# Layer 0's attention: scaling the probabilities by the merge weights, values stationary, groups summed in PSUM

## The chip, the cores and the metric

The kernel runs on one core of one Trainium2 chip. Its engines have their own instruction queues, each in order: PE (TensorE, matrix products and transposes), DVE (VectorE), ACT (ScalarE), POOL (GpSimd) and SP (SyncE, which here issues nearly all DMA transfers). The metric is the device time of one execution in microseconds.

## The reference

Two layers on 1024 tokens of width 1024: dilated attention and an MLP, then gated linear attention and an MLP. The change lies in the first layer's attention, which has 8 heads of 128 features and, for each head, three groups with their own queries, keys and values:

```python
for g, (window, dil) in enumerate(((128, 1), (512, 4), (2048, 16))):
    q = apply_rope(qkv[:, :, g, 0], cos, sin) * (HEAD_DIM ** -0.5)
    k = apply_rope(qkv[:, :, g, 1], cos, sin)
    v = qkv[:, :, g, 2]
    o_g, lse_g = dilated_group_attention(q, k, v, dil, window // dil)   # softmax over a band of keys
    outs.append(o_g); lses.append(lse_g)
alpha = jax.nn.softmax(jnp.stack(lses, axis=0), axis=0)
o = jnp.sum(alpha[..., None] * jnp.stack(outs, axis=0), axis=0)
x = x + o.reshape(B, S, ATTN_WIDTH) @ w_out
```

A group of dilation 4 or 16 attends within residue classes of the tokens (4 classes of 256 tokens, 16 of 64). The three groups' outputs are merged with weights from their softmax denominators, token by token.

## The kernel before

The projections run as products of float32 values split into a high and a low part (three matmuls of 128x512 for one product). Values are projected first and stored in DRAM (`vscr`). Then a loop over 24 passes `p` (8 heads times 3 groups, `h, g = divmod(p, NG)`) projects queries and keys. `Heads.run_head(p)` issues 14 half products of six matmuls, and calls `advance()` after each. `advance()` moves a clock by one step and issues whatever stands in an agenda for that step: `at(step, function, rank)` puts it there, lower ranks first, rank 5 where none is given. All else in the stage is placed by this agenda, in steps from `c = 14 * p`: the copies and sums of the projection's PSUM banks (`keep`, `column`), the rotary products (`turn` inside `column`, four steps after it), the rounding of the next pass's weights (`stage`), and the attention of the pass before, which `follow(p - 1, c)` plans.

In `column` a half of the queries or keys is summed on DVE, and SP then moves its two halves of partitions into each other's place (`cw`), which the rotary product needs.

Attention of one group (`Attention`; `Classes` for group 2) takes four stages, j = 0 to 3. `scores` makes query-key products with tokens of a block on partitions (at steps 8, 10, 12 and 14; group 2 makes all its 16 small ones at step 8). `soft` takes each row's extreme on DVE and the exponential with its sum on ACT (steps 9, 11, 13, 15). `turn` transposes the probabilities on PE and copies them to SBUF on ACT. `values` multiplies them, as stationary operand, with the values. The result, tokens on partitions, goes with each row's sum and extreme to DRAM (`og`, rows of 130 numbers per token and group). For group 2 `turn` stands at step 18 and `values` at step 20.

The merge of a head (`plan_merges`) starts nine steps into the pass of the next head's group 1. For each half of the tokens it reads the rows of all three groups (`merge_load`), computes three weights per token (`merge_weights`, `merge_shares`, four steps after the read), scales twelve tiles on ACT (`merge_scale`), adds them on DVE (`merge_join`), and writes the joined head to `oscr`, tokens on partitions. The output projection, which needs features on partitions, turns the joined heads again on PE: heads 0 to 3 with `turn_eight`, heads 4 to 7 with `t_head`. The last head's attention and merge (`tail`) run inside the output projection, two agenda steps per block of twelve matmuls.

PSUM has eight banks (`bank`), SBUF pools have fixed numbers of buffers: `k4` 25 of 4 KB per partition, `t2` 8, `r6` 1, `h8` 12.

Of the kernel before, what the change touches and what calls it, by code (L numbers as in the profile page):

```python
# [19 lines left out]
P = 128  # L20
D = 1024
# [20 lines left out]
def hybrid_trunk(ctx, tc, x, norm_mix, norm_mlp, norm_fin, a_in, a_out, g_in, g_up, g_b, g_nw,  # L42
# [927 lines left out]
    og = [drp.tile([S, NG, HD + 2], F32, name=f"og{h}") for h in range(HEADS)]  # L970
    oscr = drp.tile([S, D], F32, name="oscr")
# [219 lines left out]
    class Attention:  # L1191
        def __init__(self, g, h, qT, kT):
            self.g, self.h, self.qT, self.kT, self.st = g, h, qT, kT, {}

        def scores(self, j):
            ps = bank("pS").rearrange("p (i k) -> p i k", i=2)
# [5 lines left out]
            self.st[j] = ps  # L1202

        def soft(self, j):
            ps = self.st[j]
            tile_ = k4([P, 2, 512], F32, "pt")
            pt = tile_[:, 0, :].rearrange("p (i k) -> p i k", i=2)
            if j % 2 == 0:
                self.row = t2([P, 4, HD + 2], F32, "orow")
            for i in range(2):  # L1210
                k0, n, m0 = keys_of(self.g, 2 * j + i)
                r = 2 * (j % 2) + i
                m = self.row[:, r, HD + 1:HD + 2]
                dve.tensor_tensor_reduce(pt[:, i, :128 * n], ps[:, i, :128 * n], masks[:, m0:m0 + 128 * n],
                                         -scale, 1e38, op0=OP.add, op1=OP.min, accum_out=m)
                act.activation(pt[:, i, :128 * n], pt[:, i, :128 * n], AF.Exp, scale=-1.0,
                               bias=m, accum_out=self.row[:, r, HD:HD + 1])
            self.st[j] = tile_, self.row

        def turn(self, j):  # L1220
            tile_, row = self.st[j]
            pt = tile_[:, 0, :].rearrange("p (i k) -> p i k", i=2)
            ps = bank("pP")
            n = 0
            for i in range(2):
                for s in range(keys_of(self.g, 2 * j + i)[1]):
                    pe.transpose(ps[:, 128 * n:128 * n + 128], pt[:, i, 128 * s:128 * s + 128], ident)  # L1227
                    n += 1
            act.activation(tile_[:, 1, :128 * n], ps[:, :128 * n], AF.Copy)

        def values(self, j):
            tile_, row = self.st.pop(j)
            g, h = self.g, self.h
            if j % 2 == 0:
                self.po = bank("pO").rearrange("p (b d) -> p b d", d=HD)
            po = self.po
            n = 0
            for i in range(2):
                k0, nk, _ = keys_of(g, 2 * j + i)
                for s in range(nk):  # L1240
                    pe.matmul(po[:, 2 * (j % 2) + i, :], tile_[:, 1, 128 * n:128 * n + 128], self.v[:, k0 // 128 + s, :],  # L1241
                              start=(s == 0), stop=(s == nk - 1))
                    n += 1
            if j % 2:
                act.activation(row[:, :, 0:HD], po, AF.Copy)
                to = og[h][:, g, :]
                if g == 0:
                    sp.dma_start(to.rearrange("(b p) c -> p b c", p=P)[:, 2 * j - 2:2 * j + 2, :], row)
                else:
                    for n in range(2):  # L1250
                        sp.dma_start(to.rearrange("(b p r) c -> r p b c", p=P, r=4)[j - 1 + n],
                                     row[:, 2 * n:2 * n + 2, :])

        def plan(self, c, points, turn, values):

            def get():
                self.v = load_values(self.g, self.h)
            at(c + points[0] - 2, get)
            for j in range(4):
                t = c + points[j]  # L1260
                at(t, lambda j=j: self.scores(j), 2)
                at(t + 1, lambda j=j: self.soft(j), 2)
                at(c + turn[j], lambda j=j: self.turn(j), 3)
                at(c + values[j], lambda j=j: self.values(j), 4)

    class Classes(Attention):


        def scores(self, j):
            if j:  # L1270
                return
            self.ps = bank("pS").rearrange("p (b k) -> p b k", k=64)
            for b in range(8):
                for e in range(2):
                    sl = slice(128 * b + 64 * e, 128 * b + 64 * e + 64)
                    pe.matmul(self.ps[64 * e:64 * e + 64, b, :], self.qT[:, sl], self.kT[:, sl], start=True, stop=True,
                              tile_position=(0, 64 * e))
            self.pt = k4([P, 2, 512], F32, "pt")
            self.rows = [t2([P, 4, HD + 2], F32, "orow") for _ in range(2)]

        def soft(self, j):
            pt = self.pt[:, 0, :].rearrange("p (b k) -> p b k", k=64)
            for q in range(2):
                b, row = 2 * j + q, self.rows[q]
                m = row[:, j, HD + 1:HD + 2]
# [1321 lines left out]
```

## Time and profile before

| | |
|---|---|
| runs, median of 3 | 2567.89 us (2567.67 to 2568.99) |
| profiled execution, its own time | 2567.73 us |
| its span, first to last instruction | 2565.9 us |
| busy PE / DVE / ACT in the span | 2556.3 / 1863.5 / 1285.0 us |
| granted TensorE clock | 0.999 of full speed |
| DMA traffic | 544.8 MB, mean 212 GB/s |
| layer 0's heads and output projection of heads 0 to 3 | about 255 to 898 us of the span |

Times in the rows are microseconds from the span's start. A timeline row has the start, the duration, the engine, the line, the operation and its operands (out, then in). Where a row is merged, x4 counts the instructions. A float32 matmul of two operands that are not split leaves two records. Matmuls overlap, so start to start tells what one costs better than its duration. In rows of a line the three numbers are least, median and longest time in ns, and "DMA to landing" is from issue to completion in us.

### The profile page before, as it was taken

The numbers are of one execution on the slowest core, as the hardware profiler recorded it, in microseconds if no ns is written. First come the engines' busy times: TensorE is split into PE (matmuls) and PEld (weight loads), VectorE is DVE, ScalarE is ACT, GpSimd is POOL, SyncE is SP. The second block draws the span as 40 slices with busy tenths as digits, with TensorE's granted clock in tenths as the row PEclk, the third lists the DMA queues.
The fourth block names the chain that finished last, engine by engine and source line by source line (L and its number), as shares of the span: only waits on it lengthen the run. The fifth ranks groups of instructions, "written<-read, shape, count | busy, mean of one in ns | idle before, by whom it ended". The sixth has DMA issues, their size and how long they took to land.

```text
span 2565.9 us, 34655 instructions
## 1 busy us (share of the span) xinstructions
PE 2556.3 (100%) x12583; PEld 2120.2 (83%) x12583; DVE 1863.5 (73%) x2988; ACT 1285.0 (50%) x2335; POOL 17.9 (1%) x26
## 2 busy tenths in 40 slices
PE   9999999999999999999999999999999999999998
PEld 7888888888888888888888888888888888888887
DVE  7766878888888766788668785786666666566666
ACT  7443455555555445566544553654335555553344
POOL 0000000000000000000000000100000000000000
PEclk9999999999999999999999999999999999999999
DMA  5785466655656747899888765777546644495543
GB/s 191 254 276 195 108 160 151 155 152 150 161 151 189 229 164 258 265 328 307 326 302 301 278 216 195 278 252 269 182 151 216 230 149 142 154 340 205 189 147 124
DMA packets 357276, 544.80 MB, mean 212 GB/s; under 512 B 24576, under 2 KB 181008, under 8 KB 357104
## 3 DMA queue, kind: packets, MB, share of 16 engines
q1 hardware_dynamic: 356800, 542.18, 64.4%
q8 instruction: 99, 1.62, 0.3%
q14 instruction: 73, 0.60, 0.1%
q10 hardware_dynamic: 304, 0.40, 0.0%
HBM read 339.39 MB, written 177.93 MB: 202 GB/s over the span
## 4 chain that ended last, share of the span: by engine, by line
PE 99%; ACT 1%; DVE 0%; issue 0%
PE pX L854 19%; PE pB L1959 14%; PE pV L854 13%; PE pA L1959 10%; PE pB L1066 8%; PE pY L854 6%; PE pZ L854 6%; PE pA L1066 6%; PE pd L196 2%; PE pd L198 2%; PE pd L197 2%; PE pO L1241 2%; PE pS L1200 2%; PE pP L1227 1%; PE pT L259 1%; PE pO L2430 1%
## 5 line engine op out<-in xcount | busy, mean ns | idle before, releaser
L1959 PE MATMUL pB<-dh 128*128 128x512 f32 x512 | 199.2, 389 | 0.0
L1959 PE MATMUL pB<-dl,dh 128*128 128x512 f32 x512 | 199.2, 389 | 0.0
L1959 PE MATMUL pB<-dh,dl 128*128 128x512 f32 x512 | 199.2, 389 | 0.0
L205 DVE TENSOR_TENSOR dl<-sin,dh 128x1024 fp32r<-128x1024 f32 x112 | 136.6, 1220 | 62.8 <-ACT dh L202 60.2
L854 PE MATMUL pV<-s4h,wd 128*128 128x512 f32 x480 | 161.2, 398 | 0.0
L202 ACT ACTIVATE dh<-sin 128x1024 fp32r<-128x1024 f32 x112 | 117.8, 1051 | 75.1 <-PE pB L1959 33.1
L1959 PE MATMUL pA<-dh 128*128 128x512 f32 x384 | 149.6, 390 | 0.0
L1959 PE MATMUL pA<-dh,dl 128*128 128x512 f32 x384 | 149.4, 389 | 0.0
L1959 PE MATMUL pA<-dl,dh 128*128 128x512 f32 x384 | 149.4, 389 | 0.0
L859 ACT ACTIVATE e<-pX 128x512 f32<-128x512 f32 x108 | 64.5, 597 | 159.1 <-PE pX L854 158.9
L202 ACT ACTIVATE dh<-kept 128x1024 fp32r<-128x1024 f32 x64 | 67.8, 1060 | 147.0 <-DVE kept L1924 100.8
L1959 PEld LDWEIGHTS pB<-dh 128*128 128x128 f32 x512 | 96.1, 188 | 20.0
L1959 PEld LDWEIGHTS pB<-dh,dl 128*128 128x128 f32 x512 | 96.1, 188 | 20.0
L1959 PEld LDWEIGHTS pB<-dl,dh 128*128 128x128 f32 x512 | 96.1, 188 | 19.8
L854 PEld LDWEIGHTS pV<-s4h,wd 128*128 128x128 f32 x480 | 90.1, 188 | 19.2
L854 PE MATMUL pX<-s3h,wgh 128*128 128x512 f32 x240 | 96.8, 403 | 0.0
L854 PE MATMUL pX<-s2h,wbh 128*128 128x512 f32 x240 | 95.7, 399 | 0.0
L854 PE MATMUL pV<-s1h,wbh 128*128 128x512 f32 x240 | 95.6, 398 | 0.0
L854 PE MATMUL pY<-a12h,wah 128*128 128x512 f32 x240 | 95.3, 397 | 0.0
L854 PE MATMUL pX<-a11h,wah 128*128 128x512 f32 x240 | 95.0, 396 | 0.0
L854 PE MATMUL pZ<-a22h,wgh 128*128 128x512 f32 x240 | 94.8, 395 | 0.0
L854 PE MATMUL pY<-a12h,wal 128*128 128x512 f32 x240 | 93.8, 391 | 0.0
(383 smaller groups left out, 7159.7 us busy)
## 6 DMA issues: line engine op xcount, KB each, us to landing
sin<-acts SPq DMA_DIRECT2D x112, 512.0 KB, 4.6
acts<-s SPq DMA_DIRECT2D x64, 512.0 KB, 3.5
raw<-in_mlp_w_down_dram SPq DMA_DIRECT2D x64, 512.0 KB, 5.3
raw<-in_attn_w_in_dram SPq DMA_DIRECT2D x96, 256.0 KB, 4.3
cw<-c SPq DMA_DIRECT2D x192, 128.0 KB, 2.3
raw<-in_mlp_w_up_dram SPq DMA_DIRECT2D x48, 512.0 KB, 5.9
acts<-c SPq DMA_DIRECT2D x64, 256.0 KB, 2.7
kept<-in_mlp_w_down_dram SPq DMA_DIRECT2D x32, 512.0 KB, 7.0
```

Source lines behind the costliest of these rows:

```text
L196: pe.matmul(ps, sh, mh, start=start, stop=False)
L197: pe.matmul(ps, sh, ml, start=False, stop=False)
L198: pe.matmul(ps, sl, mh, start=False, stop=stop)
L202: act.activation(hi, src, AF.Copy)
L205: dve.tensor_tensor(lo, src, hi.bitcast(F32), op=OP.subtract)
L259: pe.transpose(ps[e][:, 64 * n:64 * n + 64], src[k, :], ident[k, k], tile_position=(64 * e, 0))
L854: pe.matmul(st[b], u[:, k, :], v, start=first and k + n == 0, stop=k == 3 and n == 2, skip_group_check=True)
L859: act.activation(e, self.st[p]["X"], AF.Copy)
L1066: pe.matmul(self.acc[s][t], parts[k][v == 2][:, 128 * t:128 * t + 128], (th, tl)[v == 1][:, k, :], start=fresh and m + k + v == 0, stop=m ...
L1200: pe.matmul(ps[:, i, :128 * n], self.qT[:, 128 * b:128 * b + 128], self.kT[:, k0:k0 + 128 * n], start=True, stop=True)
L1241: pe.matmul(po[:, 2 * (j % 2) + i, :], tile_[:, 1, 128 * n:128 * n + 128], self.v[:, k0 // 128 + s, :], start=(s == 0), stop=(s == nk - 1))
L1959: pe.matmul(self.acc[s][t], a[:, k, c], b[:, k, :], start=fresh and m + k + v == 0, stop=m == 7 and k == 1 and v == 2, skip_group_check=True)
```

## The change

Each row's sum and extreme (`stats`, two numbers per token and group) now go to DRAM alone, as soon as a group's `soft` is done (`send`). A head is finished by the new class `Join`, planned from the pass of the next head's group 0. It reads the stats of the three groups in the three orders in which the groups hold their rows (`begin`), computes the weights (`factors`), and scales the probabilities with them (`spread`, on ACT for groups 0 and 1, on DVE for group 2). Then it transposes them (`turn`) and multiplies with the values as the stationary operand (`values`), so that PSUM holds features on partitions and tokens in columns. Groups 0 and 1 add up in one bank; group 2 is copied to SBUF with its columns in token order (`keep_classes`) and added by DVE (`join`). `oscr` holds features on partitions, and the output projection only splits it into high and low parts (`keep_head`, `TurnedHeads`). Group 2's `soft` moves to steps 9 to 12.

```diff
-    og = [drp.tile([S, NG, HD + 2], F32, name=f"og{h}") for h in range(HEADS)]
-    oscr = drp.tile([S, D], F32, name="oscr")
+    stats = [drp.tile([S, NG, 2], F32, name=f"stats{h}") for h in range(HEADS)]
+    oscr = drp.tile([HEADS, P, S], F32, name="oscr")
...
     class Attention:
+        SOFT = 9, 11, 13, 15
+        SEND = 16
...
+        def send(self):
+            s = stats[self.h]
+            if self.g == 0:
+                sp.dma_start(s[:, 0, :].rearrange("(b p) c -> p b c", p=P), self.s)
+            else:
+                sp.dma_start(s[:, 1, :].rearrange("(b p r) c -> p r b c", p=P, r=4),
+                             self.s.rearrange("p (r b) c -> p r b c", b=2))
+
+        def spread(self, b, f):
+            t = self.block(b)
+            act.activation(t, t, AF.Copy, scale=f[:, b:b + 1])
+
+        def pieces(self, half):
+            own = lambda b: (b, len(self.keys(b)) - 1)
+            if self.g == 0:
+                lo = 4 * half
+                got = [(lo - 1, [(lo, 0)])] if half else []
+                for k in range(lo, lo + 4):
+                    got.append((k, [own(k)] + ([(k + 1, 0)] if k < lo + 3 else [])))
+                return [(k, c, 128 * (c[0][0] - lo)) for k, c in got]
+            return [(2 * r + s, [(2 * r + half, s)], r) for r in range(4) for s in range(half + 1)]
...
+        def values(self, half, po, t):
+            at_ = 0
+            for i, (k, c, where) in enumerate(self.pieces(half)):
+                n = 128 * len(c)
+                o = po[:, where:where + n] if self.g == 0 else po.rearrange("p (m r) -> p r m", r=4)[:, where, :]
+                pe.matmul(o, self.v[:, k, :], t[:, at_:at_ + n], start=self.g == 0 and i == 0, stop=True,
+                          skip_group_check=True)
+                at_ += n
...
     class Classes(Attention):
+        SOFT = 9, 10, 11, 12
+        SEND = 13
...
+        def send(self):
+            s = stats[self.h][:, 2, :].rearrange("(m n e) c -> e m n c", n=NB, e=2)
+            for e in range(2):
+                sp.dma_start(s[e], self.s[64 * e:64 * e + 64])
+
+        def spread(self, f):
+            dve.tensor_tensor(self.p, self.p, f.unsqueeze(2).to_broadcast([P, NB, 64]), op=OP.mult)
...
+    class Join:
...
+        def begin(self):
+            self.g = [groups.pop((self.h, g)) for g in range(NG)]
...
+            sp.dma_start(s[:, 0:8], f.rearrange("(b p) g c -> p b g c", p=P))
+            sp.dma_start(s[:, 8:16].rearrange("p (r b) g c -> p r b (g c)", b=2),
+                         f.rearrange("(b p r) g c -> p r b (g c)", p=P, r=4))
+            for e in range(2):
+                sp.dma_start(s[64 * e:64 * e + 64, 16:24], f.rearrange("(m n e) g c -> e m n g c", n=NB, e=2)[e])
...
+        def factors(self):
+            z = sm([P, 24], "mz")
+            e, wide = self.e, z.unsqueeze(2).to_broadcast([P, 24, NG])
+            l, m = self.s[:, :, :, 0], self.s[:, :, :, 1]
+            dve.tensor_reduce(z, m, axis=AX.X, op=OP.min)
+            dve.tensor_tensor(m, wide, m, op=OP.subtract)
+            act.activation(e, m, AF.Exp)
+            dve.tensor_tensor(l, e, l, op=OP.mult)
+            dve.tensor_reduce(z, l, axis=AX.X, op=OP.add)
+            dve.reciprocal(z, z)
+            dve.tensor_tensor(e, e, wide, op=OP.mult)
...
+        def values_classes(self):
+            t = t2([P, 512], F32, "pt")
+            act.activation(t, self.ps, AF.Copy)
+            self.po = self.g[2].values(t)
...
+        def values(self, g, half):
+            banks = self.banks.pop((g, half))
+            t = (t2 if len(banks) == 1 else k4)([P, 512 * len(banks)], F32, "pt")
+            for i, (ps, n) in enumerate(banks):
+                act.activation(t[:, 512 * i:512 * i + n], ps[:, :n], AF.Copy)
+            if g == 0:
+                self.sum = bank("pO")
+            self.g[g].values(half, self.sum, t)
...
+    def join_steps(load, first, gap=1):
+        n = lambda k: first + gap * k
+        return ((load, 5, "begin"),
+                (n(0), 9, "factors"), (n(0), 9.1, "spread", 2, None),
+                (n(1), 5, "load_values", 2), (n(1), 3, "turn_classes"), (n(1), 9, "spread", 0, range(4)),
+                (n(2), 4, "values_classes"), (n(2), 5, "load_values", 0), (n(2), 9, "spread", 1, range(0, 8, 2)),
+                (n(3), 0.5, "keep_classes"), (n(3), 3, "turn", 0, 0), (n(3), 5, "load_values", 1),
+                (n(3), 9, "spread", 0, range(4, 8)),
+                (n(4), 0.6, "values", 0, 0), (n(4), 3, "turn", 1, 0), (n(4), 9, "spread", 1, range(1, 8, 2)),
+                (n(5), 0.6, "values", 1, 0), (n(5), 3, "turn", 0, 1),
+                (n(6), 0.6, "values", 0, 1), (n(6), 0.5, "join", 0), (n(6), 3, "turn", 1, 1),
+                (n(7), 0.6, "values", 1, 1),
+                (n(8), 0.6, "join", 1))
...
-        if g == 1 and h:
-            plan_merges(h - 1, 14 * p)
+        if g == 0 and h:
+            Join(h - 1, joined).plan(14 * p, join_steps(14, 16))
...
     def tail():
         c = clock[0]
-        heads.follow(heads.count - 1, c, ((7, 7, 8, 8), (11, 11, 12, 12), (13, 13, 14, 14)))
+        heads.follow(heads.count - 1, c, (7, 7, 8, 8), (8, 8, 9, 9), 10)
+        turned.load(1)
+        Join(HEADS - 1, last_joined).plan(c, join_steps(12, 16, 2))
```

More of the change, by code (lines that the diff above doesn't have):

```diff
@@ L1220, in turn @@
[L1220 to L1258, printed above, removed]
-            for j in range(4):
[L1260 to L1264, printed above, removed]
+        def block(self, b):
+            n = 128 * keys_of(self.g, b)[1]
+            if self.g == 0:
+                return self.p[b // 4][:, b % 4, :n]
+            c = 384 * (b // 2) + 128 * (b % 2)
+            return self.p[0][:, c:c + n]
@@ new lines, in keys, with turn @@
+        def keys(self, b):
+            k0, n, _ = keys_of(self.g, b)
+            return range(k0 // 128, k0 // 128 + n)
+        def turn(self, half):
+            todo = [x for _, c, _ in self.pieces(half) for x in c]
+            banks = []
+            for i, (b, n) in enumerate(todo):
+                if i % 4 == 0:
+                    banks.append([bank("pP"), 0])
+                pe.transpose(banks[-1][0][:, 128 * (i % 4):128 * (i % 4) + 128], self.block(b)[:, 128 * n:128 * n + 128], ident)
+                banks[-1][1] += 128
+            return banks
@@ L1304, in values @@
+        def values(self, t):
+            po = [bank("pO") for _ in range(2)]
+            for n in range(8):
                 for q in range(2):
                     k = slice(64 * q, 64 * q + 64)
-                    for e in range(2):
-                        pe.matmul(self.po[q][64 * e:64 * e + 64, i, :],
-                                  self.pt[k, 1, 128 * i + 64 * e:128 * i + 64 * e + 64], self.v[k, 2 * i + e, :],
-                                  start=True, stop=True, tile_position=(64 * q, 64 * e))
@@ L1310, in values @@
-            to = og[self.h][:, 2, :].rearrange("(m j q e) c -> q e m j c", j=4, q=2, e=2)
-            for q in range(2):
-                act.activation(self.rows[q][:, :, 0:HD], self.po[q], AF.Copy)
-                for e in range(2):
-                    sp.dma_start(to[q, e], self.rows[q][64 * e:64 * e + 64])
+                    pe.matmul(po[q][:, 64 * n:64 * n + 64], self.v[k, n, :], t[k, 64 * n:64 * n + 64],
+                              start=True, stop=True, tile_position=(64 * q, 0))
@@ L1449, in merge @@
-    def merge(rows, d, e, z):
-        merge_shares(rows, d, e, z)
-        o12 = rows.rearrange("p t g c -> p (t g) c")[:, :, 0:HD]
-        dve.tensor_tensor(o12, o12, e.rearrange("p t g -> p (t g)").unsqueeze(2).to_broadcast([P, NG * 4, HD]),
-                          op=OP.mult)
-        return merge_join(rows, dve)
-    def merges(h, done):
-        rows, part = {}, {}
-        def load(half):
-            rows[half] = merge_load(h, half)
-        def start(half):
-            part[half] = merge_weights(rows[half])
-        def finish(half):
-            done(h, half, merge(rows.pop(half), *part.pop(half)))
-        return load, start, finish
+            at(c + points[0], begin, 0)
@@ L1765, in hybrid_trunk @@
             c = 14 * p
[L1766 removed]
+            at(c + 1, lambda: turned.load(0), 0)
             at(c + 3, lambda: (W.dma(), W.dma()), 0)
@@ L1852, in out_proj @@
         for tb in range(NB):
-            if tb % 2 == 0 and not layer:
-                o.turn(tb // 2 + 1)
+            if tb in (1, 2) and not layer:
+                o.turn(tb + 1)
             load_x(tb + 2)
```

214 lines of the change are left out of this document (96 added, 118 removed).

## The prediction

> **What bounds the kernel now.** I read the page's busy times first, then its chain of waits, then the engines' busy times over one head of layer 0's attention (539.7 to 615.3 us, three passes of 14 steps).
>
> ```profile
> span 2565.9 us, 34655 instructions
> PE 2556.3 (100%) x12583; PEld 2120.2 (83%) x12583; DVE 1863.5 (73%) x2988; ACT 1285.0 (50%) x2335; POOL 17.9 (1%) x26
> ...
> PE 99%; ACT 1%; DVE 0%; issue 0%
> ...
> 539.70:615.30 75.60, 75.60 (x437) 63.34 (x435) 63.74 (x140) 42.77 (x117) 0.00 (x0) 1.00 0.60 155
> ```
>
> PE owns 99% of the chain, and in the head its busy time equals the stretch: 75.60 of 75.60 us at a granted clock of 1.00. So two things alone change the time: instructions on PE, and waits that PE does not have today. Work that leaves DVE (63.74) or ACT (42.77) is worth nothing by itself. The question is then what PE reaches, and when, against what the other queues must have done by then. For that I use the timeline of PE in the pass that starts at 539.71, the one in which the head before finishes its third group (group 2).
>
> ```profile
> 553.60 1.15 PE L1276 MATMUL pS<-kT,qT 128*64 128x64 f32 x32
> ...
> 560.26 0.39 PE L854 MATMUL pZ<-a22h,wgh 128*128 128x512 f32 x1
> ...
> 567.06 0.39 PE L854 MATMUL pY<-a12h,wah 128*128 128x512 f32 x1
> ...
> 568.42 0.60 PE L1296 MATMUL pP<-ident,pt 128*128 128x128 f32 x4
> 568.78 0.48 PE L854 MATMUL pV<-s1h,wbh 128*128 128x512 f32 x1
> ```
>
> A step is half a projection product, six matmuls. The class scores are issued at step 8 (553.60), the class transposes at step 18 (568.42). Between 560.26, step 12, and 568.42 lie six steps of 1.36 us, with no attention work in them. So PE comes to step 17 at 567.06. I call these step times of that pass.
>
> **The change part by part.**
>
> *1. Transposes that go.* The joined head arrives with its 128 features on partitions, so the output projection no longer turns it on PE: eight calls of t_head (four transposes each) and four of turn_eight (16 small ones) leave.
>
> ```profile
> 862.13 0.60 PE L1489 MATMUL pT<-ident,ol 128*128 128x128 f32 x4
> 862.49 0.48 PE L196 MATMUL pd<-whi,oTh 128*128 128x512 f32 x1
> 862.81 0.39 PE L197 MATMUL pd<-wlo,oTh 128*128 128x512 f32 x1
> ...
> 873.42 0.71 PE L259 MATMUL pT<-ident,ol 64*128 64x64 f32 x16
> 874.06 0.50 PE L196 MATMUL pd<-whi,oTh 128*128 128x512 f32 x1
> ```
>
> A t_head call holds PE from 862.13 to 862.49, and the matmul behind it takes 0.32 to the next start instead of 0.23: 0.45 us. A turn_eight call holds it 0.64, plus the same 0.09: 0.73. 8 x 0.45 + 4 x 0.73 = 6.5 us saved.
>
> *2. Products with values stationary.* The number of 128-token blocks stays (15, 12, and 16 half blocks), as does that of the transposes of probabilities; group 0's 15 blocks go in nine matmuls, most 256 wide.
>
> ```profile
> 614.68 0.83 PE L1241 MATMUL pO<-v,pt 128*128 128x128 f32 x6
> 615.27 0.47 PE L854 MATMUL pX<-a11h,wah 128*128 128x512 f32 x1
> ```
>
> Three blocks (two records each) take 0.59 us now, 0.20 each, which is 5.4 for a head's 27. No row has the new form with a strided output. I bound it at 10% of that either way, 0.5 us a head, 4 over eight heads, and take nothing, because moved columns and weights are as many.
>
> *3. Work on ACT, DVE and DMA.* Per head 24 scalings, the merge's two additions per half and the [tokens, 130] rows through DRAM go. 16 scalings of probabilities, one DVE multiplication, one copy pair for the classes, and the small stats come. On SP 14 transfers a head become 10 (four sends, four reads, two writes of the joined head), and the loads of values move behind the scores. Neither engine bounds the stage; nothing taken.
>
> *4. The new wait, which decides.* Before, a head's groups were weighed after their products, with seven steps between the last write to DRAM (step 20) and the first use on DVE (step 27). Now the weights must be known before the class transposes: the third group's exponentials at step 12, send at 13, begin (four reads of all groups' stats) at 14, factors and spread at 16, transposes at 17. That is two trips through DRAM, one behind the other, and the reads wait for the writes on SP. That SP does so shows today, where a read of og waits for its own writes:
>
> ```profile
> SPq L1421 <- DMA og<-orow: 15.4, 12, 3.1
> ...
> 559.57 0.68 DVE L1342 TENSOR_TENSOR c<-pV,e 128x512 f32<-128x512 f32 x1
> ...
> 561.71 0.69 DVE L1342 TENSOR_TENSOR c<-pX,e 128x512 f32<-128x512 f32 x1
> ...
> 562.43 0.46 SPq L1343 DMA_DIRECT2D cw<-c  x1
> 562.93 0.60 SPq L1344 DMA_DIRECT2D cw<-c  x1
> ```
>
> When does send leave? The last class maxima stand on DVE behind the column addition of step 11 (559.57), so the exponentials end near 562. On SP send stands behind step 13's pair of cw transfers, which wait for a PE product and a DVE addition (561.71) and end at 563.53. Send starts then. Prices:
>
> ```profile
> L1314 SPq DMA_DIRECT2D og<-orow x32: 513/600/1500, 346.8 to 873.0; - x32
> DMA to landing us min/median/max: 2.5/2.9/5.6
> ...
> L1343 SPq DMA_DIRECT2D cw<-c x96: 461/462/527, 251.2 to 848.0; - x96
> DMA to landing us min/median/max: 2.2/2.2/7.4
> ...
> L1186 SPq DMA_DIRECT2D v<-vscr x16: 627/640/1116, 326.4 to 852.4; - x16
> DMA to landing us min/median/max: 4.0/4.6/8.5
> ...
> 359.70 0.17 DVE L1428 TENSOR_REDUCE mz<-rows 128x4 f32<-128x12 f32 x1
> ...
> 360.00 0.68 DVE L828 TENSOR_TENSOR t<-raw 128x512 f32<-128x512 f32 x1
> ...
> 361.21 0.17 DVE L1434 TENSOR_TENSOR md<-me,rows 128x12 f32<-128x12 f32 x1
> ...
> 361.91 0.68 DVE L1342 TENSOR_TENSOR c<-pZ,e 128x512 f32<-128x512 f32 x1
> ...
> L1430 ACT ACTIVATE me<-md x16: 196/212/215, 360.5 to 893.0; 128x12 f32<-128x12 f32 x16
> ...
> 363.20 0.69 DVE L1351 TENSOR_TENSOR cw<-cw,tab 128x512 f32<-128x512 f32 x1
> ```
>
> No row has pieces of 8 or 24 bytes. The write is nearest to today's class write (the same two halves of 64 partitions): second issue at 563.53 + 0.60 = 564.13, landed 2.9 later, 567.03. The four reads, 0.60 each, put the last at 568.83. Its landing lies between cw (2.2, few long pieces) and the load of values (4.6, about as many pieces): 3.4, so 572.23. The factors are today's chain of seven small operations: 0.30 (359.70 to 360.00), the exponential with its hand-overs 0.4, then 0.70 (361.21 to 361.91): 1.4. The classes' spread is a 128x512 DVE operation, 0.69. The transposes can start at 572.23 + 1.4 + 0.69 = 574.3, and PE stands there from 567.06: **7.2 us of wait a head**, for the seven heads joined inside the loop.
>
> The low end takes 2.2 for both landings and 0.51 per issue: 563.53 + 0.51 + 2.2 + 3 x 0.51 + 2.2 + 2.09 = 572.1, a wait of 5.0. The high end takes 5.6 and 4.6, with 0.64 per read: 578.3, 11.2. Nothing covers it: PE is in order, and every projection matmul of the next step is behind the transposes. Queued meanwhile: on SP the next cw pair and the weights' loads behind begin, on DVE the rotary products behind factors. They have steps of slack that the stopped PE only lengthens.
>
> By the Trainium skill, "DMA: Bandwidth & Descriptors" (the two buckets of a transfer's time), about 2 us of each transfer are fixed, mostly the receipt of the last write, so small size would not make these trips short. The trace agrees: no landing above is under 2.2. With 2.0 for both, an estimate from that page, the wait would be 5.0 and the sum 15 us smaller than mine.
>
> *5. ACT behind the restart.* The copies of turned probabilities now stand in the step of the products that use them.
>
> ```profile
> L1297 ACT ACTIVATE pt<-pP x8: 577/599/602, 342.4 to 867.5; 128x512 f32<-128x512 f32 x8
> ...
> L1216 ACT ACTIVATE pt<-pt,orow x128: 385/494/512, 274.6 to 848.6; 128x256 f32<-128x256 f32 x88, 128x128 f32<-128x128 f32 x40
> ...
> L1441 ACT ACTIVATE rows<-rows,me x168: 385/391/404, 364.0 to 867.2; 128x128 f32<-128x128 f32 x168
> ```
>
> From the factors to the products of step 20, ACT has seven wide spreads (0.49), five narrow ones (0.39), one class copy, two keeps and two copies (0.60 each): 8.4 us. It starts 0.7 before PE. PE's share of these steps is 0.4 of transposes, three products of 1.36, some 1.0 of class products and 0.8 of transposes, 6.3. So 8.4 - 0.7 - 6.3 = **1.4 us** more a head; 0 if the copies overtake the spreads' backlog, 3.5 if the key copy and the weights' rounding of step 17 also land ahead.
>
> *6. The tail.* The last head has six steps from send to factors and two per join step. Its chain of 574.3 - 563.5 = 10.8 us stands against 8 steps, 10.9 us: 2 us taken, 0 to 7.
>
> **Sum**, against the profiled execution's 2567.73 us (span 2565.9 and 1.8 around it; 0.16 under the median 2567.89): -6.5 + 7 x 7.2 + 7 x 1.4 + 2 = +55.7, **2623 us**. All low ends: -6.5 - 4 + 35 = +24.5, 2592. All high ends: -6.5 + 4 + 78 + 25 + 7 = +108, 2675.
>
> **The rivals.**
>
> *Hidden (faster).* The stats arrive before PE does, and only part 1 stays: 2567.7 - 6.5 = 2561. It decides at 6.5 / 7 = 0.9 us of wait a head. For it speaks that PE waits nowhere in this stage today. Against it: from 563.53 there are 3.5 us to 567.06, of which factors and spread take 2.1, and 1.4 us would have to hold two landings of 2.2 at least. It needs send some 6 us earlier than my reading of the queues. Chance 0.10, with another 0.06 for a wait that just cancels the gain.
>
> *The clock falls in the wait.* At the start of the kernel, coming from rest, PE ran slower.
>
> ```profile
> 6.33 1.74 PE L1066 MATMUL pB<-dh,a12h 128*128 128x512 f32 x4
> 7.91 1.08 PE L1066 MATMUL pB<-dh,a12l 128*128 128x512 f32 x4
> 8.83 1.07 PE L1066 MATMUL pB<-dl,a12h 128*128 128x512 f32 x4
> ```
>
> Four matmuls took 1.58 us from start to start at 6.33, and 0.91 at 8.83. If a wait of 7 us brings the same, the two or three steps behind it cost up to 0.17 a matmul more, 12 to 18 matmuls, 2.0 to 3.0 us a head. ACT catches up meanwhile, so it takes the place of part 5: 2623 - 9.8 + 17.5 = 2631. Chance 0.17. "TensorE: Matmul & The Clock Gate" of the Trainium skill (Part 1) states this: after an idle window of about 3.4 us the clock is halved, and about 3.4 us of work restore it. By it the loss would be 1.7 us a wait, an estimate, and 2625; no other place of this trace has such an idle time to test it.
>
> *The values' load comes last.* load_values of the classes (step 17) stands on SP behind the four reads (to 569.43) and two cw (1.06): its second transfer starts at 571.13 and lands 4.6 later, 575.7. PE needs it at 574.3 + 0.4 + 1.36 = 576.1, so it hides at the median; at the maximum of 8.5 it adds 3.5 a head, 2648. Chance 0.07.
>
> **How the numbers follow.** My forecast has 0.60, 2592 to 2655. With the clock and the load, and half of the forecast's far ends, slower holds 0.84; no change (within 0.2%, about 5 us, which is what a measurement of this kernel can tell) 0.06; faster 0.10. Leaving out the hidden case and the last ends above, the range is 2585 to 2660.
>
> **What would show it.** In the changed kernel's waits, PE (or its weight load) waits for DVE on the classes' transposes, seven times, 5 to 11 us each; today no PE wait there exists. SP waits for stats' own writes; DVE sits idle before the factors' first reduction; PE's busy share in slices 4 to 13 falls to about 8 or 9 tenths; the granted clock in these windows says if the rival holds. The t_head and turn_eight transposes are gone. Wrong I am if the stats land in under 1.5 us, or if the queues on SP or DVE run further ahead of PE than this pass shows.

## The result, and the profile after

The changed kernel takes 2686.08 us (median of 4 runs, 2681.78 to 2691.12) against 2567.78 us for the kernel before (4 runs): 1.046 times as long, 95% interval 1.0436 to 1.0485. Forecast was 2623, range 2585 to 2660: the direction is right, the size about half of the real one, and the measured time lies above the range. The profiled execution took 2681.78 us, its span is 113.6 us longer than before.

From the page of the changed kernel, the span, the busy times and the granted clock in 40 slices:

```profile
span 2679.5 us, 34003 instructions
PE 2579.6 (96%) x12391; PEld 2136.4 (80%) x12391; DVE 1855.6 (69%) x2926; ACT 1275.1 (48%) x2243; POOL 17.9 (1%) x26
...
PEclk9999998999999989999999999999999999999999
```

PE was busy for 2556.3 of 2565.9 us; now it idles for 100 us. DVE and ACT have no more to do than before. One head, from the class scores of one to those of the next (columns: length, busy us of PE, PEld, DVE, ACT, POOL with instructions, granted clock, DMA share, GB/s), and then PE's largest waits by what released them (total, times, longest):

```profile
676.10:764.60 88.50, 78.90 (x422) 65.81 (x421) 63.32 (x132) 40.61 (x102) 0.00 (x0) 0.94 0.44 97
```

```profile
PE pP L1318 <- DVE pr L1311: 80.6, 8, 12.5
PE pO L1271 <- ACT pt L1398: 3.9, 7, 2.5
PE pS L1292 <- DVE qT L1455: 3.1, 1, 3.1
```

A head was 75.60 us at clock 1.00 and is 88.50 at 0.94. L1318 is the class transposes, L1311 the classes' spread: the wait stands where the prediction put it, eight times. One of them, engine by engine (start, length, what was done; idle time before it in brackets):

```profile
598.96 0.59 SPq L1440 DMA_DIRECT2D cw<-c  x1
599.65 1.26 SPq L1308 DMA_DIRECT2D stats<-st  x2
603.81 0.37 SPq L1344 DMA_DIRECT2D stat<-stats  x1
...
604.89 1.47 SPq L1348 DMA_DIRECT2D stat<-stats  x2
...
608.09 0.23 DVE L1358 TENSOR_REDUCE mz<-stat 128x24 f32<-128x72 f32 x1 [5.34 <-DMA stat<-stats]
...
610.06 0.69 DVE L1311 TENSOR_TENSOR pr<-pr,stat 128x512 f32<-128x512 f32 x1
...
600.64 0.39 PE L854 MATMUL pY<-a12h,wal 128*128 128x512 f32 x1
610.90 1.09 PE L1318 MATMUL pP<-ident,pr 128*128 128x128 f32 x4 [9.87 <-DVE pr L1311]
```

SP sends at 599.65 and stands until the write has landed (603.81); DVE has the stats at 608.09, and PE, ready just after its last matmul of 600.64, goes on at 610.90. From send to transposes it is 11.25 us; I had forecast 10.8. But PE came to step 17 only 1.2 us after send left (0.2 to 1.7 over the seven heads), not 3.5. The same place in windows of 3 us (the granted clock is the third number from the right):

```profile
600.00:603.00 3.00, 1.03 (x5) 0.53 (x3) 2.72 (x5) 0.00 (x0) 0.00 (x0) 1.00 0.42 59
603.00:606.00 3.00, 0.00 (x0) 0.00 (x0) 0.00 (x0) 0.00 (x0) 0.00 (x0) 0.85 0.27 12
606.00:609.00 3.00, 0.00 (x0) 0.00 (x0) 0.54 (x3) 0.38 (x2) 0.00 (x0) 0.50 0.69 100
609.00:612.00 3.00, 1.10 (x5) 1.13 (x6) 2.83 (x8) 2.80 (x6) 0.00 (x0) 0.50 0.93 209
612.00:615.00 3.00, 3.00 (x12) 1.96 (x11) 2.24 (x3) 1.76 (x5) 0.00 (x0) 0.50 1.16 283
615.00:618.00 3.00, 3.00 (x35) 2.76 (x34) 2.16 (x4) 1.11 (x2) 0.00 (x0) 0.95 1.18 277
```

The clock halves in the wait and stays halved for some 4.4 us of work behind it. There a projection matmul takes 0.43 us from start to start instead of 0.23:

```profile
612.63 0.63 PE L854 MATMUL pY<-a12h,wal 128*128 128x512 f32 x1
613.06 0.63 PE L854 MATMUL pY<-a12h,wah 128*128 128x512 f32 x1
```

The last head, after the loop, waits longest:

```profile
960.60 0.38 SPq L1344 DMA_DIRECT2D stat<-stats  x1
...
963.79 2.16 SPq L133 DMA_DIRECT2D raw<-in_attn_w_out_dram  x4
...
968.71 1.06 ACT L152 ACTIVATE whi<-raw 128x1024 fp32r<-128x1024 f32 x1 [10.74 <-DMA raw<-in_attn_w_out_dram]
```

The output weights' loads, moved by the change to step 28, come behind begin on SP; ACT's rounding waits 10.74 us for them, DVE's part of it behind ACT, and factors behind that (972.85).

Where the 113.6 us are, by PE's start-to-start times summed over the trace: waits over 1.2 us +90.3 (69.2 at the seven class transposes in the loop, 18.7 in the tail); the class products +11.4 (8.3 to 19.7); the products of groups 0 and 1 +6.0; transposes of heads -5.6; projection matmuls and transposes of probabilities, which run at half clock behind the waits, +17.7; scores -4.5, whose cause I did not follow up. That makes 115 (small gaps are charged to one neighbour or the other).

### The profile page after: what moved, and what is told of

It reads as the page before. It is cut to its first block, busy times and chain, and to the rows that moved or that the text cites. A ratio compares the mean times of both kernels' runs of the same rounds, so it can differ in the third digit from the quotient of the medians.

```text
span 2679.5 us, 34003 instructions
## 1 busy us (share of the span) xinstructions
PE 2579.6 (96%) x12391; PEld 2136.4 (80%) x12391; DVE 1855.6 (69%) x2926; ACT 1275.1 (48%) x2243; POOL 17.9 (1%) x26
## 4 chain that ended last, share of the span: by engine, by line
PE 62%; ACT 0%; issue 0%; DVE 0%
PE pB L1990 13%; PE pX L854 11%; PE pA L1990 10%; PE pV L854 7%; PE pY L854 4%; PE pZ L854 4%; PE pB L1066 3%; PE pA L1066 2%; PE pd L196 2%; PE pd L198 2%; PE pd L197 2%; PE pT L259 1%; PE pO L2461 1%; PE pO L2459 0%; PE pU L2442 0%; PE pl L2229 0%
## 5 line engine op out<-in xcount | busy, mean ns | idle before, releaser
L854 PE MATMUL pY<-a12l,wah 128*128 128x512 f32 x240 | 96.7, 403 | 0.0
```

What stands on the lines that cost most here:

```text
L854: pe.matmul(st[b], u[:, k, :], v, start=first and k + n == 0, stop=k == 3 and n == 2, skip_group_check=True)
```

## The experiments

Theory A at the start: the wait is a fixed time, two trips to DRAM and the factors, and more steps between begin and transposes hide it. Each edit below is against the changed kernel; "class waits" are those at the seven class transposes inside the loop, 9.2 to 11.2 us there, 9.9 on average (PE's time from start to start, less the 0.22 us that a matmul takes). Step lists are shortened: entries stand without their neighbours. Runs 1 to 10 were executed once each, and the changed kernel's four runs spread over 9 us, so I read no difference of that size between their times; what counts is the waits in the traces.

**1. and 2. Transposes three steps later, and eight** (the second with 24 for 19).

```
-            Join(h - 1, joined).plan(14 * p, join_steps(14, 16))
+            Join(h - 1, joined).plan(14 * p, join_steps(14, 19))
```

> All steps of the join from factors on stand three steps later (17 becomes 20 for the class transposes); the sends and the reads of stats stay. Theory A (the weights are ready at a fixed time after step 12, PE comes too early): the wait before the class transposes falls by 3 x 1.36 = 4.1 us in each of seven heads, from 10.0 to about 5.9, and the run from 2682 to about 2653 us. Rival B (the chain moves along with the join steps, because DVE or ACT reach it late whenever it stands): the wait stays near 10 us and the run near 2682.

> The same, eight steps later. Theory A: 8 x 1.36 = 10.9 us of slack exceeds the wait of 10.0, so the wait is 0 to 1 us, the granted clock stays at full, and some 7 x (10 + 2) = 84 us go: about 2598 us, with the last head's waits in the output projection (some 19 us) left. Rival B: near 2682. Rival C (probabilities held longer make the next passes wait for buffers): the class wait goes, but other waits of PE come up in the loop, and the run stays above 2630.

Measured: 2688.04 and 2707.16 us; class waits 8.1 to 9.7 and 9.3 to 10.2. Theory A, which forecast class waits of 5.9 and of 0 to 1, falls: the wait moves along. With eight steps more, SP and then DVE, around 710 us:

```profile
702.91 1.25 SPq L1308 DMA_DIRECT2D stats<-st  x2
707.21 0.37 SPq L1344 DMA_DIRECT2D stat<-stats  x1
...
709.77 0.57 SPq L1439 DMA_DIRECT2D cw<-c  x1
...
711.03 2.27 SPq L1430 DMA_DIRECT2D raw<-in_attn_w_in_dram  x4
...
719.28 0.69 DVE L1447 TENSOR_TENSOR cw<-cw,tab 128x512 f32<-128x512 f32 x1 [3.85 <-DMA cw<-c]
724.12 0.22 DVE L1358 TENSOR_REDUCE mz<-stat 128x24 f32<-128x72 f32 x1
```

While SP stands before begin (to 707.21), the next swap of rotary halves (cw) and the next group's weights (raw) stand behind it. They land late, DVE waits for cw at 719.28, and factors, later in DVE's order, start at 724.12 though their stats landed some 12 us before. From here on theory Q: the wait is the order of the in-order queues, SP's and then DVE's; rival D: it is the trips.

**3. No trip to wait for.** Heads 1 to 6 read the stats of the head before (their merge weights are another head's), at step 10.

```
-            f = stats[self.h]
+            f = stats[self.h - 1 if 0 < self.h < HEADS - 1 else self.h]
...
-join_steps(14, 16)
+join_steps(10 if h > 1 else 14, 16)
```

> Heads 1 to 6 take their merge weights from the stats of the head before, read four steps earlier (step 10), so no read waits for a fresh write; the computation of those weights is that of another head, all work is the same. Theory A in its parts: DVE can start the factors when its queue reaches them (602.7 instead of 608.1 in the head shown), so six waits fall by about 5.3 us to some 4.6, which belong to DVE's lag, factors and spread: about 2650 us. If the two trips were the whole wait: six waits of 0, about 2615. If the trips were not the cause: 2682.

Measured: 2654.62 us; class waits 4.1 to 5.2 in those heads, 9.8 in the first. The trips, with what they hold up on SP, are 5 us of the wait; the other half is DVE's lag, the factors and the spread (594.18 to 596.8 there, right behind DVE's other work).

**4. PE kept busy.** 32 more transposes' worth of matmuls on data that is not used, ahead of the class transposes.

```
+            for i in range(32):
+                pe.matmul(ps[:, :128], ident, ident, start=True, stop=True)
```

> 32 float32 matmuls of the identity with itself (about 0.22 us each, 7.2 us) stand on PE ahead of the class transposes of each head, whose bank they write first; nothing reads them. They fit into the wait of 10 us. Clock theory (the wait lets the granted clock fall to half, which costs about 2 us behind each wait): the transposes start when they do now, the clock stays at 1.00 behind them, and eight times 2 us go: about 2666 us. Rival (what follows the wait is slow for another reason): 2682, and the matmuls behind the wait still take 0.43 us from start to start.

Measured: 2667.70 us, 14.1 less in the span than the profiled execution of the changed kernel, with *more* work on PE. From one head's class transposes to the next is 1.7 us less on average inside these two traces. Behind the transposes (607.46 in this kernel) the clock is full:

```profile
608.00:611.00 3.00, 3.00 (x35) 2.45 (x36) 2.96 (x5) 2.02 (x6) 0.00 (x0) 1.00 1.20 274
```

So the clock that falls in the wait cost about 2 us a head. It still fell in the first, the third and the last head of this run, so 14.1 us is not all of it.

**5. and 6. Begin at step 18, transposes at 25; then the values' loads early too** (the lower part of the edit).

```
-join_steps(14, 16)
+join_steps(18, 24)
...
-(n(1), 5, "load_values", 2), (n(2), 5, "load_values", 0), (n(3), 5, "load_values", 1)
+(load, 5.1, "load_values", 2), (load + 2, 5, "load_values", 0), (load + 4, 5, "load_values", 1)
```

> Join steps eight later, as in the run with eight steps, and begin four steps later as well (step 18 instead of 14), behind the pass's weight loads on SP. Theory A' (a blocked queue: begin stands on SP waiting for the writes of stats, and holds back the cw transfers and the weights' loads behind it; their lateness makes DVE and ACT late, so the wait moves along with the join): the writes have landed when SP reaches begin, cw and the loads leave as early as before, and the wait of 10 us at the class transposes goes. What comes next are the values, whose loads stand one step ahead of their use: up to 4.5 us at the class products. About 2640 us. Theory C (buffers held too long): class wait stays near 10 us, 2700.

> The same, and the loads of values of groups 2, 0 and 1 stand at steps 18, 20 and 22 (12, 14 and 16 in the tail). Theory A': no wait over 1 us of PE is left in the loop, the granted clock stays at 1.00, and the tail's waits of some 19 us are what remains with the slower class products: 2567.4 - 6.5 + 8 x 0.9 + 19 + a few = about 2590 us. Theory C: above 2640, with waits for buffers.

Measured: 2683.84 and 2689.67 us, class waits 5.3 to 9.7 and 8.6 to 12.6. Both forecasts missed. In the first, PE idles 14 us less than in the changed kernel, but PE's waits for values come instead (9.5 us in ten waits) and the granted clock is lower (0.979 over the span for 0.982), so no time is won. In the second, SP has the reads right behind the weights' loads of step 17:

```profile
693.69 2.22 SPq L1430 DMA_DIRECT2D raw<-in_attn_w_in_dram  x4
...
696.50 2.96 SPq L1345 DMA_DIRECT2D stat<-stats  x1
699.51 1.97 SPq L1348 DMA_DIRECT2D stat<-stats  x2
701.58 1.28 SPq L1186 DMA_DIRECT2D v<-vscr  x2
702.96 0.59 SPq L1439 DMA_DIRECT2D cw<-c  x1
```

Issuing a read there takes up to 2.96 us instead of 0.62, and the swap of step 19 leaves at 702.96; DVE then stands 6.50 us for it, factors (712.64) behind. No read waits for a write here any more; in this head what is late is late by its place on SP.

**7. Class products and the tail.** As four 64x64 tiles instead of two of 64x128, and the output weights' loads back at step 8.

```
+                    for e in range(2):
+                        d = slice(64 * e, 64 * e + 64)
+                        pe.matmul(po[q][d, 64 * n:64 * n + 64], self.v[k, n, d], ..., tile_position=(64 * q, 64 * e))
...
-        at(c + 28, weights)
+        at(c + 8, weights)
```

> Two separate edits. (1) The class products as four tiles of 64x64 instead of two of 64x128: if the wide tile's pace of 108 ns per pair is the stationary side, the 32 records' stretch at full clock falls from 1.75 to about 0.9 us, as before the change, 7 us in all. Rival: the pace is the moving side, and the stretch stays or grows (twice the instructions). (2) In the tail the weights of the output projection's second half are asked for at step 8 (as before the change) instead of behind step 12's begin: theory A' says that the tail's wait of 12.7 us at the class transposes comes from these loads standing behind begin on SP, with ACT and DVE waiting for them ahead of the factors, so it falls to some 4 us or less. Rival (the last head's own chain): it stays over 10 us. Together 2682 - 7 - 9 = about 2666 us.

Measured: 2654.82 us. The tail's class wait went from 12.7 to 4.5 us. Class products sum to 11.1 us over the trace instead of 19.7, 1.1 us in a head at full clock and up to 1.9 where it is halved. The time is 11 us below the forecast; part of that is that the class waits in the loop also fell, to 9.1 on average, which the forecast did not have and I did not follow up. One head's class products:

```profile
343.80 1.16 PE L1328 MATMUL pO<-pt,v 64*64 64x64 f32 x64
```

**8. Sends of groups 0 and 1 at step 21 instead of 16**, away from the weights' loads of step 17.

```
-        SEND = 16
+        SEND = 21
```

> Only the sends of the statistics of groups 0 and 1 move, from step 16 to step 21 of their plan: out of the place between the swap of step 1 and the weight loads of step 3, into the stretch of steps 6 to 10 in which SP issues nothing else. Class sends, begin and transposes stay. Theory Q (the 1024 small pieces of a send, ahead of the weight loads on the DMA queues, make the loads and the swaps behind them late, so that DVE and ACT lag the products and the class statistics leave late): the loads of raw land after 4.3 us again instead of 5.6, DVE's column add of step 13 falls back beside PE's step 13 (2.3 us earlier), the seven waits at the class transposes shrink from 9.9 to about 7.5 us, and the time is 2660 to 2670 us. Rival F (DVE and ACT lag because the new layout gives them more to do between the swaps, whatever the queues hold): waits stay at 9.5 to 10, time 2678 to 2688.

Measured: 2673.05 us, between the two forecasts, class waits 8.3 to 8.9: 1.2 less on average, where theory Q had forecast 2.4. Its first half holds. Of the loads of raw, first in the changed kernel, then here, who waited and the time to landing:

```profile
  ACT wah L791: 10.2, 13
DMA to landing us min/median/max: 3.0/5.6/9.1
```

```profile
  ACT wah L791: 2.5, 2
DMA to landing us min/median/max: 2.9/4.3/5.8
```

Send now leaves 2.5 us ahead of PE's step 17 in all seven heads, against 1.3 on average in the changed kernel and the 3.5 of the prediction. The 1.0 us that is still missing is not the queues'. One head from its class scores on, with ACT's copy of a projection bank, DVE's column addition of step 13 that waits for it, and the send:

```profile
579.16 1.15 PE L1292 MATMUL pS<-kT,qT 128*64 128x64 f32 x32
...
587.61 0.57 ACT L1475 ACTIVATE e<-pX 128x512 f32<-128x512 f32 x1
588.22 0.69 DVE L1438 TENSOR_TENSOR c<-pX,e 128x512 f32<-128x512 f32 x1 [0.42 <-ACT e L1475]
...
590.13 1.26 SPq L1308 DMA_DIRECT2D stats<-st  x2
```

The addition starts 9.06 us after the class scores, in all seven heads; in the kernel before it was 8.11 (553.60 to 561.71 in the prediction's rows, and 8.1 in five of the seven heads). ACT makes that copy right behind the classes' exponentials, and the change itself moved these forward: four of the eight maxima and exponentials stood ahead of that addition before, all eight do now. The swap of step 13 waits for the addition, and the send stands behind the swap. So rival F, more work on DVE and ACT between the swaps, is right for this part.

**9. Everything of the join in SP's free stretch.** Begin behind the swap of step 19, values' loads at 20, 21, 22, class transposes at 25.

```
-join_steps(14, 16)
+join_steps(19, 24)
...
-(n(1), 5, "load_values", 2), (n(2), 5, "load_values", 0), (n(3), 5, "load_values", 1)
+(n(1) - 5, 5, "load_values", 2), (n(2) - 5, 5, "load_values", 0), (n(3) - 5, 5, "load_values", 1)
```

> begin moves from step 14 to step 19, behind the swap of that step on SP, the three loads of values follow at steps 20, 21 and 22, and factors, spread and class transposes move from 16, 16, 17 to 24, 24, 25. So everything that the join issues on SP stands in the stretch between the swaps of steps 19 and 25, in which SP has nothing else to issue, and the sends of step 13 have landed long before begin asks for them. Theory Q (the waits at the class transposes are what the join's reads and loads do to the swaps and weight loads behind them on SP, plus two trips to DRAM): no swap is late, factors are done before step 25, the seven class waits are 0 to 3 us each, the clock stays at 1.0 there, and the time is 2595 to 2620 us. Rival D (the join needs its two DRAM trips and in-order queues of DVE and ACT wherever it stands, as in the four runs that moved it): waits of 6 us or more stay, 2640 to 2690 us.

Measured: 2645.47 us, class waits 3.6 to 7.2: better than any other place so far, 25 us above theory Q's range and inside rival D's, though six of the seven waits are below D's 6 us. SP holds little up now (DVE waits 0.54 us for a swap in the head shown). What is left is on DVE:

```profile
679.66 0.69 DVE L792 TENSOR_TENSOR wal<-raw,wah 128x512 fp32r<-128x512 f32 x1
...
682.20 0.22 DVE L1358 TENSOR_REDUCE mz<-stat 128x24 f32<-128x72 f32 x1
...
684.15 0.69 DVE L1311 TENSOR_TENSOR pr<-pr,stat 128x512 f32<-128x512 f32 x1
```

Four operations on weights (2.5 us from 679.66), factors 2.0, spread 0.7, and one step between factors and transposes: PE was ready at 681.1.

**10. and 11. Run 9 with factors ahead of the work on weights, transposes a step later; then with 7, 8 and a later tail** (the last two pairs of lines).

```
-(n(0), 9, "factors"), (n(0), 9.1, "spread", 2, None)
+(first - 1, 6.5, "factors"), (first - 1, 6.6, "spread", 2, None)
...
-join_steps(19, 24)
+join_steps(19, 25)
...
-        heads.follow(heads.count - 1, c, (7, 7, 8, 8), (8, 8, 9, 9), 10)
+        heads.follow(heads.count - 1, c, (9, 9, 10, 10), (10, 10, 11, 11), 12)
...
-        Join(HEADS - 1, last_joined).plan(c, join_steps(12, 16, 2))
+        Join(HEADS - 1, last_joined).plan(c, join_steps(14, 20, 2))
```

> As the run that begins at step 19 (2645.5 us, class waits 4.9 us), with one change of order: factors and the classes' spread stay at step 24, but stand ahead of the rounding of weights on DVE instead of behind it (2.4 us earlier on DVE), and the class transposes and all behind them move from step 25 to 26 and on; the spreads of groups 0 and 1 on ACT keep their old steps, so that they are a step further ahead of the copies of turned probabilities. Theory Q (no trip to DRAM is left in the wait; what is left is DVE's order with one step between factors and transposes): the class waits fall to 0 to 1.5 us, the waits of 1.6 us at the first products of groups 0 and 1 to under 0.5, no half clock, 2590 to 2605 us. Rival R (DVE is too full in these steps: what factors no longer wait for comes back as late weights or late swaps at another place on PE): waits of 2 us or more a head elsewhere, 2610 to 2640 us.

> The same, with all that the other runs point to: sends of groups 0 and 1 at step 21, class products as four 64x64 tiles (8.6 us less PE time in the run that had them), the output weights' loads of the tail at step 8, and the tail's last head two steps later (scores 9, send 12, begin 14, factors 20) with the first half's sum joined a step before the next copies on ACT. Theory: loop 2590 to 2605 minus 8.6 for the tiles and 14 to 18 for the tail, 2565 to 2580 us: the attention stage is then as dense on PE as before, the 6.5 us of turned heads are gone, and what is left above 2561 is in the tail. Rival: the tail has no spare work on PE to put in front of the last head's chain, so its waits stay at 10 us or more: 2580 to 2600.

Measured: 2672.19 us, and 2633.68 us (1.0259 times before, 1.0242 to 1.0276), both above every range that was forecast. The class waits in the loop are 0 to 2.7 and 0 us, near what theory Q has; the time is not. PE's first wait of each, from the two lists:

```profile
PE pO L1326 <- ACT pt L1385: 54.2, 7, 7.8
```

```profile
PE pO L1328 <- ACT pt L1387: 52.6, 7, 7.8
```

The class products now wait almost 8 us a head for ACT's copy of the turned classes. By the shift of one step it stands in step 27, behind that step's softmax exponentials, which wait for DVE; and DVE waits (2.81 us in one head of run 10) for an ACT copy that stands behind eight scalings. Rival R, work that comes back as a wait elsewhere, was right, though not by weights or swaps.

**12. That copy ahead of the exponentials**, products at step 29, scalings and products of groups 0 and 1 up to step 36.

```
+(26, 3, "turn_classes"), (27, 0.6, "copy_classes"), (27, 9, "spread", 0, range(4)),
+(29, 4, "values_classes"), (30, 0.5, "keep_classes"), (30, 9, "spread", 0, range(4, 8)),
+(31, 3, "turn", 0, 0), (31, 9, "spread", 1, range(0, 8, 2)),
+(32, 0.6, "values", 0, 0), (33, 3, "turn", 1, 0), (33, 9, "spread", 1, range(1, 8, 2)),
```

> The run before it had no wait left at the class transposes but 8 us a head at the class products, for the copy of the turned classes on ACT, which stood in step 27 behind that step's softmax exponentials (they wait for DVE). Here the copy stands ahead of them on ACT (rank 0.6 of step 27) and the products two steps behind it (step 29); the spreads of groups 0 and 1 go to steps 27, 30, 31 and 33, and the products of the two groups to steps 32 to 36, where ACT has no softmax; the tail's join stands two steps later still. Theory Q (PE pays only where an in-order engine has less than its own backlog between its operation and PE's use): PE waits under 2 us a head in the loop, the clock stays at 1.00, and the time is 2562 to 2580 us, level with before or up to 1% above. Rival R (the scalings of 128 x 2816 probabilities a head are more than ACT and DVE can place anywhere in this head without holding up scores, swaps or weights): waits of 3 us or more a head turn up in yet another place, 2590 to 2640 us.

Measured: 2609.00 us, 1.0162 times before (1.0148 to 1.0175), in rival R's range. One wait is left, 3.6 to 4.2 us in each head of the loop: a copy behind two groups of scalings.

```profile
PE pO L1271 <- ACT pt L1402: 28.4, 8, 4.2
```

**13. The last wait taken up.**

```
+(31, 0.6, "copy", 0, 0), (31, 9, "spread", 1, range(0, 8, 2)),
+(32, 0.6, "values", 0, 0), (33, 3, "turn", 1, 0),
+(34, 0.6, "values", 1, 0), (34, 9, "spread", 0, range(4, 8)),
+(35, 3, "turn", 0, 1), (35, 9, "spread", 1, range(1, 8, 2)),
```

> The last version (2609.0 us) with its one remaining wait in the loop taken up: 4.3 us a head at step 32, where the copy of group 0's turned probabilities stood on ACT behind two groups of scalings. The copy of (group 0, first half) goes to step 31, ahead of them, the scalings of group 0's second half and of group 1's odd blocks to steps 34 and 35, the products they feed to 36 and 37; in the tail the classes' values are loaded two steps behind begin. Theory Q (what is left is only order; the layout itself costs PE nothing): PE's idle time is under 1.5 us a head, the granted clock 1.00 from 330 us to 900 us, the period of a head 75.5 to 77.5 us against 75.6 before, 2563 to 2580 us. Rival R (the layout cannot be hidden in this loop: another wait of 2 us or more a head appears, or the sum of PE's own work in a head is above 77 us without waits and at full clock): 2585 to 2610 us.

Measured: 2564.89 us (11 runs) against 2567.69 (15 runs), ratio 0.9988, interval 0.9979 to 0.9997, as theory Q has it. The clock over its span, a head, PE's largest wait, and a class transpose:

```profile
PEclk9999999999999999999999999999999999999999
```

```profile
634.00:709.90 75.90, 75.90 (x456) 63.53 (x456) 63.58 (x134) 40.20 (x102) 0.00 (x0) 1.00 0.49 113
```

```profile
PE pO L1271 <- ACT pt L1402: 2.3, 5, 0.7
```

```profile
725.12 0.69 DVE L1311 TENSOR_TENSOR pr<-pr,stat 128x512 f32<-128x512 f32 x1
...
726.26 0.60 PE L1318 MATMUL pP<-ident,pr 128*128 128x128 f32 x4
```

The same layout, trips, scalings and copies take a head of 75.9 us, against 75.6. So the 118 us of the change were order, and the clock and tile form that the next section sizes; the layout itself saves about 0.1%.

## Why the prediction was half right

*What bounds the kernel: right.* PE's busy time filled the stage, and the loss came as PE waits. That DVE's and ACT's busy times fell a little was worth nothing; part 3, which took their work at 0, overlooked its order.

*Part 1, transposes that go: right.* -5.6 us where I had -6.5.

*Part 2, products: groups right, classes mis-sized.* I took nothing, 4 either way. Groups 0 and 1 measured +6.0, in part at half clock, and about +3.5 in run 13 without waits. The class products' new tile form (64x128, 64 columns) was taken as free; it cost 11.4 us over the trace. Part of that is the half clock; where the clock was mostly full (run 9) the sum is 15.6, which is 0.12 us for each of a head's 16 matmuls, against 0.065 in the old form (64x64 tiles, 128 columns) and 0.9 us a head. The row of the old form was in the trace, and I did not price the change of form.

*Part 4, the wait: right in place and mechanism, 9.9 instead of 7.2.* The chain from send to transposes was within 0.5 us (11.25 for 10.8), in part by luck: in the head shown the last read took 2.4 us to reach DVE where I had 3.4, the factors 2.0 where I had 1.4, and the write some 0.6 more. The term that failed is the lead: I read from the trace of before that send leaves 3.5 us ahead of PE's step 17, and it left 1.2 ahead there, 1.3 on average. That reading kept the queues of before. The change makes them late in two ways: sends of 1024 small pieces stand ahead of weights and swaps (run 8: 1.2 us), and all of the classes' maxima and exponentials, moved to steps 9 to 12, stand ahead of the column addition of step 13, which I had left at 561.71 (1.0 us, in run 8's trace). The prediction's own list of what it would be wrong by names the queues, with the wrong sign: they ran further behind, not ahead.

The sentence that failed more deeply is "they have steps of slack that the stopped PE only lengthens", on the swaps, weights and rotary products queued meanwhile. Runs 2 and 6 show that this slack is what the wait eats: what delays them delays factors, in the same order on DVE. As a result I would have called more steps the cure, and runs 1 and 2 say no.

*Part 5, ACT: right as a mechanism, hidden here.* I had 1.4 us a head; the copies at the products of groups 0 and 1 cost PE 3.9 us in all, 2.5 of them in the tail. Presumably ACT caught up during the longer wait. A copy held up on ACT appeared once that wait was gone: almost 8 us a head in runs 10 and 11, by way of DVE, and directly behind the scalings, as part 5 has it, some 4 us in run 12.

*Part 6, the tail: 2 forecast, 0 to 7; 18.7 measured.* I counted steps for the trips and did not follow the moved `weights` step (8 to 28) on SP. 8.2 us of it go in run 7; class scores (3.3) and the last copy (2.7) wait on DVE's and ACT's order.

*The rivals.* The clock rival held: run 4 gives 14.1 us, about 2 a head, the low end of the 2 to 3 I had worked out from the kernel's start. It got a chance of 0.17 because the trace had no idle place to test it; with a wait of 7 us as the forecast itself, it should have been part of the forecast. "TensorE: Matmul & The Clock Gate" of the Trainium skill (Part 1) says this: halved after about 3.4 us without work, restored after about as much work. The trace agrees in kind: here the clock fell 4.1 us after PE's last matmul and came back 4.4 us after it restarted. In other places it does not keep to 3.4: the clock fell 2.2 us after PE's last matmul in run 9, and at 429 us of the changed kernel it came back only after 11.9 us. The values' load hid in the changed kernel (it showed in run 5, about 1 us a head). "Hidden" was refuted at this place and order, and run 13 shows its time, 2564.9 for 2561, at another.

*The sum.* Forecast -6.5 + 50.4 + 9.8 + 2 = +55.7. Measured: -5.6 for transposes, +69.2 for the loop's waits, +18.7 for the tail's, +17.4 for products, +17.7 for what ran at half clock and small waits, -4.5 for scores, 113 together. The range's high end had no room for three terms at once: clock, tile form and tail.

## What to carry to other kernels

A wait that a change adds is not priced by its own chain alone: look at what stands behind the waiting instruction on each in-order queue, and whether the operation that ends the wait stands behind that in turn; if it does, moving the wait later gains little (run 1: 1.2 of 4.1 us a head on average; run 2: 0.1 of 10.9). Put the whole exchange (send, read, use) where its queue is idle, one engine after the other, and read the list of waits again after each move, since the next engine's order shows only then. A wait of a few microseconds on PE costs its length and then the clock behind it; 3.5 us was enough here.

## What the runs showed of the hardware that I had not expected

- The clock is lost sooner and for longer than one place suggests: in run 9 it fell 2.2 us after PE's last matmul (wait 3.5 us at 430) and came back 5.6 us after the restart; in run 12 2.8 and 6.1; in the changed kernel 4.1 and 4.4, and at its second wait (429 us) it came back only 11.9 us after the restart, with PE busy all that time.
- The issue of one DMA of 1024 small pieces on SP took 0.62 us with SP's queue free and 2.96 right behind four weight loads (run 6).
- Small pieces as such were cheap: an 8-byte packet held a DMA engine for 7 ns, a 24-byte one for 9, a 520-byte one for 28 (medians). What they cost was their own landing (4.1 and 5.8 us for the two sends of 1024 pieces, 3.2 for those of 512) and the loads behind them: landing after 5.6 us instead of 4.3 (medians).
